# Even-layer attention heads: key low parts computed once, joined diagonals, a split pool of output-weight slabs and an earlier-issued gated product

## The chip, the cores and the metric

The kernel runs on one core of a Trainium2 chip. A core has a matrix engine (TensorE, PE in the profile), a vector engine (VectorE, DVE), a scalar engine (ScalarE, ACT), GpSimd (POOL) and a sync engine (SP) from which nearly all DMAs here are issued. Each engine works through its own instructions in a fixed order and waits on semaphores for the others. The metric is the device time of one launch in microseconds, taken as the median of the runs; lower is better. A profile of one execution stands beside it.

## The reference

Two layers over 512 tokens of width 1024 and 256 context tokens. Layer 0 is the "even" mixer with a feed-forward block, layer 1 the "odd" one with another. The change lies in the even mixer:

```python
def diff_attn(q, k, v, lam):                 # 4 heads, each with two score maps c = 0, 1
    s = jnp.einsum('bqhd,bkhd->bhqk', q, k).astype(jnp.float32) * ATTN_SCALE
    p = jax.nn.softmax(s, axis=-1).reshape(b, B_HEADS, 2, tq, tk)
    a = p[:, :, 0] - lam * p[:, :, 1]
    return jnp.einsum('bhqk,bkhe->bqhe', a.astype(v.dtype), v)

def diff_out(o, g, lam_init):
    return (rmsnorm(o, g) * (1.0 - lam_init)).reshape(b, t, B_V_WIDTH)

y = jnp.concatenate([chunk_mlp(u, v, w_s, b_s), diff_out(o, subln_g, lam_init)], axis=-1) @ w_out
```

The 512 tokens see 512 + 256 keys, the 256 context tokens see the 256 context keys only. `chunk_mlp` is a gated product: `u = gelu(h @ w)` times a mixed, normalized `gelu` of the other half. All is in float32.

## The kernel before

**Numbers in two parts.** Matrix products take operands rounded to a shorter float (F32R). So each operand is split into a rounded high part and a low part, the rest, and a product is three matmuls: high by high, high by low, low by high (`mm3`, lines 115 to 117). `split` and `unit` make the parts: ACT casts the high part, DVE or POOL subtracts it for the low part.

**The heads.** A score map has 64 channels, so high and low part of a query stand in the two halves of the 128 partitions of one tile (`stack_q`). The key tiles hold the same 64 channels in both halves: `stack_k` (line 281) makes a tile `kh` with the high part twice and a tile `kl` with the low part twice, and the score is query tile times `kh` plus query tile times `kl`. Each of the two maps of a head has its pair, so a head has four key tiles and four DVE subtractions (line 290) of 64 partitions by 768 columns. `softmax_diff` (line 537) does one block of 128 queries: two score maps into PSUM, a row maximum each (DVE, line 550), an exponential each (ACT, line 552, with the row sums), then on DVE the reciprocal, a factor (557), the difference of the two maps (558), and an epsilon term of the later norm, EPS times the squared sum (559). `attend` takes two such blocks, transposes them on PE (570), splits them into `ath` and `atl` (131, 132) and multiplies them with the values. A head has three `attend`, so six blocks. `norm` does the RMS norm of a head in steps: squares (ACT), sums by matmuls with ones and the reciprocal root on DVE with six small diagonal matrices (`rstd_diag`, lines 165 to 187), and a matmul that spreads the diagonals plus a scaling (615). The norm of head t-1 runs inside head t; that of head 3 stands at the end.

**What runs beside the heads.** The heads are traced with a high priority. PE's remaining time is filled with other products: `block` projects queries and keys of the later heads, with `rope` (line 260, DVE and POOL), and `gated` the four u products. Each `gated` is 24 matmuls over 512 columns and 24 over 256, into the one PSUM bank of `fill`. The framework orders each engine's instructions by priority along a timeline that it simulates; `issue_after(x)` forces an instruction behind `x` on its engine. For `gated(3, self.last_sum)` on line 704 all but the first two of the eight steps of the 512-column product (`dense`, `first = 2`) are put behind the last head's sums.

**What follows.** The weights `even_out` are loaded as eight slabs of 512 KB (`slab`, order 4, 5, 6, 0, 1, 2, 3, 7). Each takes a raw tile (three buffers), a cast on ACT (line 89) and a subtraction on POOL (line 92) into a slot of 8 KB per partition. All eight slots belong to one pool, opened after the ring of the earlier weights is closed; it reuses memory of the earlier ring, of the rope tables and of the attention tiles, and each tile waits until the tiles it lies on are released. The concatenated inputs `cat` are split in the same stretch into tiles that the inputs of `gated` held before. Then `xT` and `ctxT` are reloaded (line 43), the feed-forward weights begin to load (832), and `project(0, range(8), ...)` runs 24 matmuls for each slab in that order into eight accumulators.

Of the kernel before, what the change touches and what calls it, by code (L numbers as in the profile page):

```python
# [18 lines left out]
TC = 256  # L19
TA = TX + TC  # L20
HID = 2816
NF = HID // P
EPS = 1e-6
ROOT = 0.703952253
# [3 lines left out]
class Builder:  # L28
# [230 lines left out]

    def rope(self, ps, out, tabs):  # L260
        nc = self.nc
        sh = self.ropep.tile([P, 512], F32, name=self.uid("sh"), tag="sh", bufs=self.sh_bufs)
        nc.vector.stream_shuffle(sh, ps, ROT)
        nc.vector.tensor_tensor(out, ps, tabs[0], ALU.mult)  # L264
        nc.gpsimd.tensor_tensor(sh, sh, tabs[1], ALU.mult)
        nc.gpsimd.tensor_tensor(out, out, sh, ALU.add)
# [11 lines left out]
                nc.vector.scalar_tensor_tensor(lo[Y], q[X], s, hi[X].bitcast(F32), ALU.mult, ALU.subtract)  # L278
        return qa, qb

    def stack_k(self, k, pool, T, tag, bufs):
        nc = self.nc
        out = []
        for X, Y in ((slice(0, 64), slice(64, 128)), (slice(64, 128), slice(0, 64))):
            kh = pool.tile([P, T], F32R, name=self.uid("kh"), tag=tag, bufs=bufs)
            kl = pool.tile([P, T], F32R, name=self.uid("kl"), tag=tag, bufs=bufs)
            nc.scalar.copy(kh[X], k[X])
            nc.scalar.copy(kh[Y], k[X])
            for Z in (X, Y):
                nc.vector.tensor_tensor(kl[Z], k[X], kh[X].bitcast(F32), ALU.subtract)  # L290
            out.append((kh, kl))
        return out

# [39 lines left out]
    def even(self):  # L333
        tc, nc, a = self.tc, self.nc, self.a
        self.open_ring(512, 5, 6)
        self.ropep = tc.alloc_tile_pool(name="rope0", bufs=1, side="left", reuse_waits="tile")
        self.sh_bufs = 1
        self.ropep.tile([P, 512], F32, name=self.uid("sh"), tag="sh", bufs=1)
# [12 lines left out]
        for k in range(0, KT, 2):  # L351
            t = self.load(Rh, a["xT"][k * P:(k + 2) * P, :].rearrange("(k p) t -> p k t", p=P), [P, 2, TX], f"hx{k}")
# [47 lines left out]
        sq = self.squares(hx, TX)  # L400
        slabs = sum([ada_load(1, 1, k) for k in range(0, KT, 2)], [])
# [23 lines left out]
        qk = {}  # L425
# [37 lines left out]
        W = []  # L463
# [73 lines left out]
        def softmax_diff(Q, K, qb, eps):  # L537


            koff = 0 if qb < 4 else TX  # L540
            qs = slice(qb * P, (qb + 1) * P)
            nm, sums = self.small(2, "sa", 10), self.small(2, "sa", 10)
            es = []
            for c in range(2):
                ps = self.wide()
                for p in range(2):
                    if qb < 4:
                        nc.tensor.matmul(ps[:, :TX], Q[c][:, qs], K[c][p][:, :TX], start=p == 0, stop=p == 1)
                    nc.tensor.matmul(ps[:, TX:TA], Q[c][:, qs], K[c][p][:, TX:], start=p == 0, stop=p == 1)
                nc.vector.tensor_reduce(nm[:, c:c + 1], ps[:, koff:TA], axis=AX, op=ALU.max, negate=True)  # L550
                e = Ra.tile([P, TA], F32, name=self.uid("e"), tag="e", bufs=6)
                self.last_exp = nc.scalar.activation(e[:, koff:], ps[:, koff:TA], AF.Exp, bias=nm[:, c:c + 1],
                                                     accum_out=sums[:, c:c + 1])
                es.append(e[:, koff:])
            r = self.small(1, "sa", 10)
            nc.vector.reciprocal(r, sums[:, 1:2])
            nc.vector.scalar_tensor_tensor(r, r, self.nlam, sums[:, 0:1], ALU.mult, ALU.mult)
            nc.vector.scalar_tensor_tensor(es[0], es[1], r, es[0], ALU.mult, ALU.add)
            nc.vector.scalar_tensor_tensor(eps[:, qb:qb + 1], sums[:, 0:1], EPS, sums[:, 0:1], ALU.mult, ALU.mult)
            return es[0]  # L560

        def attend(t, Q, K, qp, o, eps):
# [21 lines left out]
        def gated(i, after=None):  # L584

            W = self.blocks(a["uv"][i])
            u = f3() if i < 4 else f3("rv")
            for off, T, A in ((0, TX, axx), (TX, TC, axc)):
                ps = (self.fill if off or i < 4 else self.bank)()[:, :T]
                self.dense(ps, W, A, after, 0 if off else 2)  # L590
                nc.scalar.copy(u[:, off:off + T], ps)
            raw[i] = u

        def stack(t):
            return (self.stack_q(qk[t], Ra, TA, "sq", 3, eng=nc.gpsimd if t == 3 else nc.vector),
                    self.stack_k(qk[4 + t], Ra, TA, "sk", 6))

        norms = {}

        def norm(t, step):  # L600

            if t not in norms:
                return
            o, eps = norms[t][:2]
            if step == 0:
                sq = self.sumsq()
                nc.scalar.activation(sq, o, AF.Square)
                norms[t] = o, eps, sq
            elif step == 1:
                sq = norms[t][2]  # L610
                norms[t] = o, eps, self.rstd_diag([(sq[:, :TX], TX), (sq[:, TX:], TC)], 1.0 / P, eps=eps)
            else:
                for off, T, dg in ((0, TX, norms[t][2][0]), (TX, TC, norms[t][2][1])):
                    c = o[:, off:off + T]
                    nc.vector.scalar_tensor_tensor(c, c, self.subg, self.spread(dg), ALU.mult, ALU.mult)

        def head(t):
            Q, K = QK.pop(t)
            o = f3("o", 4)
            eps = self.small(6, "sx", 2)  # L620
            for qp in range(3):
                attend(t, Q, K, qp, o, eps)
                if qp == 0:
                    norm(t - 1, 1)
                elif qp == 1:
                    if t < 3:
                        QK[t + 1] = stack(t + 1)
                    norm(t - 1, 2)
            norms[t] = o, eps
            norm(t, 0)  # L630
            if t == 3:
                norm(t, 1)
                norm(t, 2)
            oraw.append(o)
# [1198 lines left out]
```

## Time and profile before

| | us |
|---|---|
| median of three runs | 1580.58 |
| lowest, highest | 1578.69, 1582.02 |
| the profiled execution, whole | 1577.26 |
| its span in the profile | 1575.4 |

The profile names an instruction by line, engine, operation and tiles: `sa<-pw` reads a PSUM tile `pw` and writes a tile with the tag `sa`. In a table of windows each row gives a stretch of the span, the busy time of each engine in it, the clock granted to TensorE (1.00 is full speed) and the DMA share. In a table of groups, the two numbers behind the bar are the busy time of the group in all and the mean duration of one instruction in ns. In a timeline, the first number is the start, the second the duration, and the bracket gives the idle time before it and who ended it. The heads run from about 164 to 322 us, the last gated product and the first half of the output projection from there to about 373 us.

### The profile page before, as it was taken

How to read it: one execution, taken by the hardware profiler on the slowest of the kernel's cores; microseconds unless marked ns; L12 is line 12 of the kernel's file. 1: busy time of each engine (PE TensorE's matmuls, PEld its weight loads, DVE VectorE, ACT ScalarE, POOL GpSimd, SP SyncE). 2: the span in 40 equal slices, each digit the busy share in tenths (PEclk: the TensorE clock that was granted, in tenths of full speed). 3: DMA queues.
4: the chain of work that ended last, by engine and by line, in shares of the span. 5: the costliest groups of instructions: out<-in, count | busy, mean ns of one | idle time of the engine just before them, and what ended most of it. 6: DMA issues, size and time to landing. Idle time of an engine off the chain costs nothing.

```text
span 1575.4 us, 25009 instructions
## 1 busy us (share of the span) xinstructions
PE 1514.1 (96%) x9563; PEld 1354.2 (86%) x9563; DVE 1079.9 (69%) x1938; ACT 726.3 (46%) x1489; POOL 826.5 (52%) x558
## 2 busy tenths in 40 slices
PE   6999999889999999999999999999999999999998
PEld 4767888779999999999999988777879889999997
DVE  4613888853697787888886487665667966666665
ACT  2415566633653333333333354565655644444444
POOL 0452331041337767767776534541314399898982
PEclk9999999989999999999999999999999999999999
DMA  9772100042223333345442211210225133333201
GB/s 356 289 251 70 45 14 1 1 157 110 68 71 111 112 110 127 126 138 172 163 157 93 82 41 61 68 34 11 72 83 184 56 100 105 104 100 108 96 21 54
DMA packets 53415, 162.26 MB, mean 103 GB/s; under 512 B 6192, under 2 KB 8624, under 8 KB 45616
## 3 DMA queue, kind: packets, MB, share of 16 engines
q1 hardware_dynamic: 46240, 135.37, 25.3%
q10 hardware_dynamic: 7056, 25.30, 4.9%
q8 instruction: 75, 1.23, 0.3%
q14 instruction: 44, 0.36, 0.1%
HBM read 158.55 MB, written 2.10 MB: 102 GB/s over the span
## 4 chain that ended last, share of the span: by engine, by line
PE 79%; DVE 14%; ACT 2%; issue 2%; DMA 2%; POOL 0%; SPq 0%; DVEq 0%; ACTq 0%; POOLq 0%
PE pw L115 10%; PE pw L116 10%; PE pw L117 10%; PE pb L116 8%; PE pb L117 8%; PE pb L115 8%; PE pf L115 3%; PE pf L116 3%; PE pf L117 3%; PE pb L1643 2%; PE pb L1632 2%; PE pf L373 2%; PE pw L1594 1%; DMA raw<-even_out 1%; PE pw L1602 1%
## 5 line engine op out<-in xcount | busy, mean ns | idle before, releaser
L115 PE MATMUL pw<-ax,w 128*128 128x384 f32 (+2 forms) x716 | 227.4, 320 | 7.8 <-ACT w L89 4.2
L793 DVE SCALAR_TENSOR_TENSOR xT<-pb,mod,xT 128x512 f32<-128x512 f32 (+3 forms) x204 | 143.1, 709 | 129.2 <-PE pb L117 128.8
L116 PE MATMUL pw<-ax,w 128*128 128x384 f32 (+2 forms) x716 | 227.8, 318 | 3.5 <-DVE ax L49 2.2
L117 PE MATMUL pw<-ax,w 128*128 128x384 f32 (+2 forms) x716 | 227.4, 319 | 0.6 <-POOL w L92 0.3
L92 POOL TENSOR_TENSOR w<-raw,w 128x512 fp32r<-128x512 f32 (+1 forms) x78 | 116.2, 1496 | 196.7 <-ACT w L89 195.0
L49 POOL TENSOR_TENSOR w<-raw,w 128x512 fp32r<-128x512 f32 x122 | 185.4, 1535 | 48.9 <-ACT w L49 48.8
L49 POOL TENSOR_TENSOR w<-t,w 128x512 fp32r<-128x512 f32 x99 | 148.8, 1506 | 56.2 <-ACT w L49 56.2
L115 PE MATMUL pb<-hh,w 128*128 128x512 f32 x480 | 171.4, 357 | 1.2 <-DVE xT L793 1.2
L117 PE MATMUL pb<-hh,w 128*128 128x512 f32 x480 | 171.7, 358 | 0.0
L116 PE MATMUL pb<-hh,w 128*128 128x512 f32 x480 | 171.6, 357 | 0.0
L115 PE MATMUL pw<-T,w 128*128 128x384 f32 (+1 forms) x508 | 156.6, 310 | 2.5 <-DVE hs L999 1.2
L116 PE MATMUL pw<-T,w 128*128 128x384 f32 (+1 forms) x508 | 157.0, 310 | 1.2 <-DVE T L132 1.2
L117 PE MATMUL pw<-T,w 128*128 128x384 f32 (+1 forms) x508 | 157.0, 310 | 0.0
L115 PE MATMUL pf<-ax,w 128*128 128x256 f32 (+2 forms) x460 | 150.0, 326 | 1.1 <-DVE qf L264 1.1
L117 PE MATMUL pf<-ax,w 128*128 128x256 f32 (+2 forms) x460 | 148.5, 323 | 0.0
L116 PE MATMUL pf<-ax,w 128*128 128x256 f32 (+2 forms) x460 | 148.2, 322 | 0.0
L115 PEld LDWEIGHTS pw<-ax,w 128*128 128x128 f32 x716 | 136.0, 191 | 13.2 <-ACT w L89 5.0
L116 PEld LDWEIGHTS pw<-ax,w 128*128 128x128 f32 x716 | 136.7, 191 | 8.6 <-DVE ax L49 2.7
L117 PEld LDWEIGHTS pw<-ax,w 128*128 128x128 f32 x716 | 136.6, 191 | 3.7 <-POOL w L92 1.5
L49 POOL TENSOR_TENSOR hh<-hs,hh 128x768 fp32r<-128x768 f32 (+1 forms) x42 | 77.8, 1854 | 92.5 <-ACT hh L49 91.0
L49 POOL TENSOR_TENSOR w<-rawo,w 128x512 fp32r<-128x512 f32 x59 | 104.0, 1762 | 28.4 <-ACT w L49 28.4
L240 DVE SCALAR_TENSOR_TENSOR junk<-ar,cb 128x1024 bf16<-128x1024 f32 x64 | 106.8, 1668 | 0.0
(415 smaller groups left out, 3923.3 us busy)
## 6 DMA issues: line engine op xcount, KB each, us to landing
raw<-ffn_in SPq DMA_DIRECT2D x44, 1024.0 KB, 5.4
ar<-ada SPq DMA_DIRECT2D x24, 1024.0 KB, 6.7
ar<-ada ACTq DMA_DIRECT2D x48, 512.0 KB, 3.6
rawo<-ffn_out SPq DMA_DIRECT2D x88, 256.0 KB, 3.0
raw<-odd_out SPq DMA_DIRECT2D x28, 256.0 KB, 2.6
raw<-qk SPq DMA_DIRECT2D x16, 256.0 KB, 4.6
raw<-uv SPq DMA_DIRECT2D x16, 256.0 KB, 3.3
raw<-even_out SPq DMA_DIRECT2D x8, 512.0 KB, 4.9
```

Of the source, the lines that this page charges most:

```text
L49: self.tail[key] = fn(*args, **kw)
L92: eng.tensor_tensor(lo, raw, hi.bitcast(F32), ALU.subtract)
L115: mm(out, s[0], m[0], start=start, stop=False, **kw)
L116: mm(out, s[0], m[1], start=False, stop=False, **kw)
L117: return mm(out, s[1], m[0], start=False, stop=stop, **kw)
L240: return self.nc.vector.scalar_tensor_tensor(junk, t, 1.0, self.cb[who], ALU.mult, ALU.mult, accum_out=self.acc[who][:, col:col + 1])
L373: nc.tensor.matmul(ps[32 * q:32 * q + 32, :w], cst[:, k, :], t[:, w * q:w * q + w], start=k == 0, stop=k == KT - 1, skip_group_check=True)
L793: ins = self.nc.vector.scalar_tensor_tensor(h, ps[:, r], self.modcol(l, j, m, who), h, ALU.mult, ALU.add)
L1594: nc.tensor.matmul(ps[:, st:en], Q, K[g][p][:, b0 * P:b1 * P], start=p == 0, stop=p == 1, skip_group_check=True)
L1602: last = nc.tensor.matmul(ps[:, en:en + TC], Q, K[g][p][:, TX:], start=p == 0 and not edge, stop=p == 1, skip_group_check=True)
L1632: last = nc.tensor.transpose(pt[:, x * P:(x + 1) * P], es[2 * (x % 2) + x // 2][:, kb * P:(kb + 1) * P], self.ident)
L1643: nc.tensor.matmul(po[64 * h:64 * h + 64, :], V[vb][:, 64 * g:64 * g + 64], t[:, h * TC:h * TC + TC], start=kb == 0, stop=kb == nb - 1, sk ...
```

## The change

- `stack_k` computes each low part once, in the half of the partitions in which the query's high part stands; the other half, which met the query's low part, is zero, so the product of low by low is left out. The four `kl` tiles are allocated once for even and odd heads, their zero halves are written by four GpSimd memsets before the first head, and `kh` has three buffers of its own.
- The row sums of all six blocks of a head are kept in one tile of 12 columns. A new `head_diag` takes the place of `rstd_diag` in `norm`: one epsilon operation for all six blocks, a reciprocal root with two steps and tuned constants instead of three, and two diagonal operations with broadcast operands (four and two blocks) instead of six.
- In `gated(3, ...)` the first five of eight steps of the 512-column product are free of the order behind the last sums, instead of two.
- The eight slab slots are split: six in a pool `slabs`, two in the ring that also holds the raw tiles. The two are taken by the first two slabs. Both pools are released at the same place as before.
- `rope` uses a scratch tile of the shared tag "t" (two buffers) in the even layer instead of a tile of its own (one buffer), and `sgub` lies in a buffer of the tag "o".

```diff
-    def stack_k(self, k, pool, T, tag, bufs):
+    def stack_k(self, k, pool, T, tag, bufs, lows):
...
+        for X, Y, kl in zip((slice(0, 64), slice(64, 128)), (slice(64, 128), slice(0, 64)), lows):
             kh = pool.tile([P, T], F32R, name=self.uid("kh"), tag=tag, bufs=bufs)
-            kl = pool.tile([P, T], F32R, name=self.uid("kl"), tag=tag, bufs=bufs)
             nc.scalar.copy(kh[X], k[X])
             nc.scalar.copy(kh[Y], k[X])
-            for Z in (X, Y):
-                nc.vector.tensor_tensor(kl[Z], k[X], kh[X].bitcast(F32), ALU.subtract)
+            nc.vector.tensor_tensor(kl[X], k[X], kh[X].bitcast(F32), ALU.subtract)
...
-        sh = self.ropep.tile([P, 512], F32, name=self.uid("sh"), tag="sh", bufs=self.sh_bufs)
+        sh = self.ropep.tile([P, 512], F32, name=self.uid("sh"), tag="sh", bufs=2) if self.sh_bufs else self.tmp("t")
...
-            sgub = self.load(Rv, a["sgub"].partition_broadcast(P), [P, 512], "sgub")
+            sgub = f3("o", 4)[:, :512]
+            nc.sync.dma_start(sgub, a["sgub"].partition_broadcast(P))
...
-            nm, sums = self.small(2, "sa", 10), self.small(2, "sa", 10)
+            nm, sums = self.small(2, "sa", 10), sums[:, 2 * qb:2 * qb + 2]
...
-            nc.vector.scalar_tensor_tensor(eps[:, qb:qb + 1], sums[:, 0:1], EPS, sums[:, 0:1], ALU.mult, ALU.mult)
...
-                self.dense(ps, W, A, after, 0 if off else 2)
+                self.dense(ps, W, A, after, 0 if off else (2, 5)[i == 3])
...
+        lows = [[Ra.tile([P, TA], F32R, name=f"kl{i}{c}") for c in range(2)] for i in range(2)]
+        for i in range(2):
+            nc.gpsimd.memset(lows[i][0][64:128].bitcast(F32), 0.0)
+            nc.gpsimd.memset(lows[i][1][0:64].bitcast(F32), 0.0)
...
-                    self.stack_k(qk[4 + t], Ra, TA, "sk", 6))
+                    self.stack_k(qk[4 + t], Ra, TA, "kh", 3, lows[t % 2]))
...
+        def head_diag(sq, sums):
+
+            ve = nc.vector
+            v, y, u = self.small(6), self.small(6), self.small(6)
+            s0 = sums[:, :12].rearrange("p (n c) -> p n c", c=2)[:, :, 0]
+            ve.scalar_tensor_tensor(u, s0, EPS, s0, ALU.mult, ALU.mult)
+            for o, n in ((0, 4), (4, 2)):
+                ps = self.bank()
+                for j in range(n):
+                    c = slice(j * P, (j + 1) * P)
+                    self.last_sum = nc.tensor.matmul(ps[:, c], sq[:, (o + j) * P:(o + j + 1) * P], self.ones, start=j == 0,
+                                                     stop=True, skip_group_check=True)
+                col = ps[:, :n * P].rearrange("p (j f) -> p j f", f=P)[:, :, 0]
+                ve.scalar_tensor_tensor(v[:, o:o + n], col, 1.0 / P, u[:, o:o + n], ALU.mult, ALU.add)
+            ve.tensor_scalar(y.bitcast(I32), v.bitcast(I32), -0.5, float(0x5F1FFFF9), ALU.mult, ALU.add)
+            ve.tensor_tensor(u, y, y, ALU.mult)
+            ve.scalar_tensor_tensor(u, u, -1.0, v, ALU.mult, ALU.mult)
+            ve.scalar_tensor_tensor(y, u, 2.38924456, y, ALU.add, ALU.mult)
+            ve.tensor_tensor(u, y, y, ALU.mult)
+            ve.scalar_tensor_tensor(u, u, ROOT * ROOT, v, ALU.mult, ALU.mult)
+            ve.scalar_tensor_tensor(u, u, -10.0 / 3.0, u, ALU.add, ALU.mult)
+            ve.scalar_tensor_tensor(y, u, 5.0, y, ALU.add, ALU.mult)
+            dgs = []
+            for o, n in ((0, 4), (4, 2)):
+                dg = self.tmp()[:, :n * P]
+                self.last_diag = ve.scalar_tensor_tensor(
+                    dg.rearrange("p (j f) -> p j f", f=P), y[:, o:o + n].unsqueeze(2).to_broadcast([P, n, P]), 0.375 * ROOT,
+                    self.ident.unsqueeze(1).to_broadcast([P, n, P]), ALU.mult, ALU.mult)
+                dgs.append(dg)
+            return dgs
...
-        self.open_ring(1024, 3, 8)
-        slots = [self.slot() for _ in range(KT)]
+        self.slabs = tc.alloc_tile_pool(name="slabs", bufs=1, side="left", reuse_waits="tile")
+        slots = [self.slabs.tile([P, 2, 1024], F32R, name=self.uid("w"), tag="w", bufs=6) for _ in range(KT - 2)]
+        self.open_ring(1024, 3, 2)
+        slots += [self.slot() for _ in range(2)]
...
         self.close_ring()
+        if both:
+            self.slabs.release()
```

More of the change, by code (lines that the diff above doesn't have):

```diff
@@ L336, in even @@
         self.ropep = tc.alloc_tile_pool(name="rope0", bufs=1, side="left", reuse_waits="tile")
-        self.sh_bufs = 1
-        self.ropep.tile([P, 512], F32, name=self.uid("sh"), tag="sh", bufs=1)
+        self.sh_bufs = 0
         tabs = [self.ropep.tile([P, TX], F32, name=n, tag=n, bufs=1) for n in ("cos", "sin")]
@@ L535, in even, with softmax_diff @@
         oraw, raw = [], {}
-        def softmax_diff(Q, K, qb, eps):
+        def softmax_diff(Q, K, qb, sums):
             koff = 0 if qb < 4 else TX
             qs = slice(qb * P, (qb + 1) * P)
-            nm, sums = self.small(2, "sa", 10), self.small(2, "sa", 10)
+            nm, sums = self.small(2, "sa", 10), sums[:, 2 * qb:2 * qb + 2]
             es = []
@@ L610, in norm @@
                 sq = norms[t][2]
-                norms[t] = o, eps, self.rstd_diag([(sq[:, :TX], TX), (sq[:, TX:], TC)], 1.0 / P, eps=eps)
+                norms[t] = o, eps, head_diag(sq, eps)
             else:
@@ L619, in head @@
             o = f3("o", 4)
-            eps = self.small(6, "sx", 2)
+            eps = self.small(12, "sx", 2)
             for qp in range(3):
```

1 line of the change is left out of this document (removed).

## The prediction

> **What bounds the kernel now.** I read the page's head first, then the table of windows over the stretch that the change touches, then what TensorE waited for in it.
>
> ```profile
> span 1575.4 us, 25009 instructions
> PE 1514.1 (96%) x9563; PEld 1354.2 (86%) x9563; DVE 1079.9 (69%) x1938; ACT 726.3 (46%) x1489; POOL 826.5 (52%) x558
> ```
>
> TensorE is busy 96% of the span, and the change removes no matmul. So time can only come from TensorE's idle time and from stretches in which its clock is granted at half.
>
> ```profile
> 164.00:300.00 136.00, 127.59 (x816) 112.82 (x814) 121.69 (x280) 87.31 (x185) 32.14 (x22) 1.00 0.05 15
> 300.00:308.00 8.00, 6.52 (x49) 5.76 (x49) 6.71 (x27) 5.75 (x15) 0.00 (x0) 1.00 0.01 2
> 308.00:312.60 4.60, 0.78 (x4) 0.31 (x2) 3.92 (x8) 3.07 (x5) 0.00 (x0) 0.69 0.00 0
> 312.60:317.00 4.40, 4.40 (x15) 3.46 (x16) 2.15 (x10) 0.37 (x1) 0.00 (x0) 0.55 0.00 0
> 317.00:322.70 5.70, 3.35 (x25) 2.63 (x23) 1.88 (x4) 1.80 (x3) 0.00 (x0) 1.00 0.29 86
> ...
> 331.20:334.80 3.60, 0.03 (x1) 0.03 (x1) 2.45 (x2) 3.59 (x6) 2.68 (x3) 0.84 0.00 0
> 334.80:340.40 5.60, 5.60 (x18) 5.60 (x19) 5.60 (x3) 4.02 (x5) 5.60 (x2) 0.50 0.25 83
> 340.40:373.30 32.90, 31.80 (x176) 30.05 (x174) 8.64 (x6) 9.11 (x10) 16.88 (x7) 1.00 0.60 225
> 373.30:420.00 46.70, 46.70 (x277) 46.43 (x277) 29.91 (x76) 20.71 (x48) 14.56 (x12) 1.00 0.16 53
> ```
>
> Columns: stretch, length, busy time of TensorE, weight loads, VectorE, ScalarE, GpSimd, granted clock, DMA. Idle TensorE: 136.00 - 127.59 = 8.4 us up to 300, then 1.5, 3.8 and (317 to 322.7) 2.35, together 16.1 us in the heads; 3.6 us before the projection and 1.1 us in it. Clock: at 0.55 for 4.4 us about 2.0 us are lost, at 0.50 for 5.6 us 2.8 us. VectorE is busy 89% of the first stretch. From 373.3 TensorE has no idle time for 47 us, so what is won before then is not given back there.
>
> ```profile
> PE pb L116 <- DVE atl L132: 5.4, 7, 2.0
> PE pw L115 <- ACT w L89: 3.6, 1, 3.6
> PE pb L115 <- ACT ath L131: 3.5, 3, 2.5
> ...
> PE pb L668 <- DVE rv L669: 1.7, 1, 1.7
> ```
>
> These are TensorE's waits from 164 to 335 us (total, count, longest). The largest is for a VectorE operation, the low part of the transposed softmax; the second is a single wait, for the cast of the first output slab.
>
> **Part 1, VectorE's work in the heads.** Its groups from 164 to 322 us, and the two joined diagonals that already exist at the seam of the layers:
>
> ```profile
> L290 DVE TENSOR_TENSOR kl<-f,kh 64x768 fp32r<-64x768 f32 x12 | 12.4, 1031 | 0.5 <-ACT kh L287 0.3
> L559 DVE SCALAR_TENSOR_TENSOR sx<-sa 128x1 f32<-128x1 f32 x24 | 6.8, 285 | 0.8 <-ACT e L552 0.8
> ...
> L185 DVE TENSOR_SCALAR q<-ident,sm 128x128 f32<-128x128 f32 x18 | 3.8, 283 | 0.1
> ...
> L146 DVE TENSOR_TENSOR sm<-sm 128x6 f32<-128x6 f32 x9 | 2.5, 276 | 0.1
> ...
> L148 DVE SCALAR_TENSOR_TENSOR sm<-sm,sm 128x6 f32<-128x6 f32 x9 | 1.5, 162 | 0.1
> ...
> L147 DVE SCALAR_TENSOR_TENSOR sm<-sm,sm 128x6 f32<-128x6 f32 x9 | 1.4, 155 | 0.0
> ```
> ```profile
> L49 DVE SCALAR_TENSOR_TENSOR q<-sm,ident 128x512 f32<-128x512 f32 x1 | 0.7, 694 | 0.0
> ...
> L49 DVE SCALAR_TENSOR_TENSOR q<-sm,ident 128x256 f32<-128x256 f32 x1 | 0.4, 425 | 0.0
> ```
>
> Low parts: 6 of the 12 go, 6 x 1.03 = 6.2 us. Epsilon: 24 x 0.285 = 6.8 us become 4 operations of the six-column kind, 4 x 0.16 = 0.65 us; 6.2 us less. Root: ten small operations a head become eight; at the mean of their rows, (276 + 162 + 155) / 3 = 198 ns, that is 0.4 us, three norms in the stretch, 1.2 us. Diagonals: 3.8 us (18 that overlap one another) become 3 x (0.69 + 0.43) = 3.4; 0.4 us. Together 14 us of VectorE.
>
> [...]
>
> How much of 14 us reaches the end? At most TensorE's 8.4 us of gaps up to 300, at least nothing, because ScalarE's exponentials and casts stand in the same chain. The waits on `atl` and `rv` (7.1 us) are VectorE's, and removed operations stand in its queue ahead of them. I take 5 us, nearer the upper end. Bounds 0 and 8.4.
>
> **Part 2, the freed matmuls.** The gated product of index 3 after the last sums, first and last of 18:
>
> ```profile
> 322.68 0.48 PE L115 MATMUL pf<-ax,w 128*128 128x512 f32 x1
> ...
> 326.63 0.40 PE L117 MATMUL pf<-ax,w 128*128 128x512 f32 x1
> ```
>
> 18 matmuls in (326.63 - 322.68) x 18 / 17 = 4.2 us, so 0.232 us each. Nine of them may now run earlier: 2.1 us. The idle time from 300 to 322.7 is 7.65 us, so there is room. After the last sums only nine remain, and the second half of the product follows 2.1 us sooner. The diagonals must then be ready sooner too: two small operations fewer (0.4 us) and a first diagonal that no longer waits for four single ones cover about half of this, and the copy of the first half out of its bank covers the rest. I take 2.1 us. Below: if the nine stand in TensorE's queue ahead of scores that are ready, they delay the chain by 2.1 us, so -2.1. Above: if they break up the gaps after 308, the 2.0 us at half clock come on top, 4.1.
>
> [...] The trace has the clock at half after gaps of 2.46 and 1.36 us in a row (308 to 312.6), so here the measurement decides. [...]
>
> **Part 3, the slabs.**
>
> ```profile
> 319.89 1.28 SPq L86 DMA_DIRECT2D raw<-even_out  x3
> ```
> ```profile
> DMA to landing us min/median/max: 3.5/4.9/11.9
> ```
> ```profile
> 327.12 0.59 ACT L591 COPY f<-pf 128x512 f32<-128x512 f32 x1 [5.85 <-PE pf L117]
> ...
> 333.68 1.04 ACT L89 CAST w<-raw 128x1024 fp32r<-128x1024 f32 x1
> ```
>
> Three raw slabs are asked for at 319.89 and land within about 5 us (landing times of the `even_out` loads). ScalarE is idle for 5.85 us until 327.1 and yet casts the first slab at 333.68, after the gated product has ended. I read this as the slot: the eight slots reuse, among others, the memory of the ring whose weights the gated product still reads, and the first slab is given one of these. In the split pool the first two slabs have slots of their own above, on attention tiles, which are free about when the raw slabs come. Then both casts fit into ScalarE's gap and both subtractions on GpSimd begin some 9 us sooner, and the 3.6 us wait and the 2.8 us of half clock behind it go.
>
> But the end of this stage hangs on the last slab:
>
> ```profile
> 349.38 0.41 SPq L86 DMA_DIRECT2D raw<-even_out  x1
> ...
> 355.57 0.33 SPq L86 DMA_DIRECT2D raw<-even_out  x1
> ```
> ```profile
> 367.51 1.05 ACT L89 CAST w<-raw 128x1024 fp32r<-128x1024 f32 x1 [4.20 <-DMA raw<-even_out]
> ```
> ```profile
> SPq L43 <- DVE ax L132: 6.2, 1, 6.2
> ```
> ```profile
> L132 DVE TENSOR_TENSOR ax<-f,ax 128x768 fp32r<-128x768 f32 x4 | 11.6, 2945 | 1.9 <-ACT ax L131 1.9
> ...
> L725 DVE TENSOR_TENSOR f<-f,rv 128x768 f32<-128x768 f32 x1 | 0.9, 946 | 0.0
> ```
> ```profile
> L92 POOL TENSOR_TENSOR w<-raw,w 128x1024 fp32r<-128x1024 f32 x8 | 22.5, 2827 | 14.7 <-ACT w L89 14.7
> ```
>
> The sixth and eighth slab are issued at 349.38 and 355.57, behind the reloads of `xT`, whose memory SP gets only when VectorE has split the last inputs. Those subtractions take 2945 ns while GpSimd subtracts slabs at the same time; one of the same size, in the same stretch, takes 946. If two of GpSimd's (2 x 2.8 us) are done before, one or two of VectorE's run at the short price, 2 to 4 us. So the whole train of loads moves by about 3 us beyond parts 1 and 2, and with it the last cast. Upper bound: with no slab late, 192 matmuls at 32.9 / 190 = 0.173 us take 33.2 us from 331.2, ending at 364.4 in place of 373.3, 8.9 us. Lower bound 0, as TensorE just waits longer for the sixth to eighth slab. I take 3.
>
> **Edits at nothing.** Four memsets on GpSimd of 64 by 768:
>
> ```profile
> L357 POOL MEMSET cst<- 128x256 f32 x1 | 0.3, 317 | 0.0
> ...
> L265 POOL TENSOR_TENSOR sh<-sh,sin 128x512 f32<-128x512 f32 x18 | 25.2, 1403 | 59.9 <-DVE sh L263 38.7 <-DVE sa L556 9.6 <-DVE mv L655 8.0
> ```
>
> At 0.3 us (three times as many columns would be 1.0) to 1.4 us each they are 1.3 to 5.6 us, before the first scores at 164 and beside a GpSimd that is busy 32 of 136 us after that. Without this cover the first head would start by that much later. The rope's two shared buffers remove a wait of VectorE on GpSimd and add none that I find, since no other user of the tag runs in the heads. The move of `sgub` leaves its DMA in the same place of SP's queue; head 3's output takes that buffer over when the mixing has long read it.
>
> **The sum.** 5 + 2.1 + 3 = 10.1 us. The profiled execution took 1577.26, its span 1575.4, and the median of the runs is 1580.58, 3.3 us above it. The forecast is 1577.26 - 10.1 = 1567.2 on the profile's own scale and 1570.5 on that of the median. A difference under 0.2% (3.2 us) can't be told from no change.
>
> **The rivals.** (Times on the median's scale.)
>
> *The slabs gain nothing.* The slot was not what held the cast, or the last slab comes as late as before, and half of part 1 is hidden: 3 + 2 = 5 us, 1575.5. For it: the DMA stretch before the last slab is already full, and ScalarE's queue may place the casts where they are. Against: ScalarE's 5.85 us of idleness with the data landed.
>
> *All gaps close.* 8.4 + 4.1 + 6 = 18.5 us, 1562. For it: VectorE's removed 14 us exceed TensorE's gaps. Against: 3.5 us of waits are for ScalarE's `ath`, behind three GELUs that stay.
>
> *TensorE is not freed.* The chain runs through ScalarE as soon as VectorE is quicker, the freed matmuls only change places, and the slabs wait for DMA: about 2 us, 1578.6, no change.
>
> *The shared tile of sums makes it slower.* The exponential of a block writes its row sums into the tile that VectorE reads for the block before. If waits are placed by tile and not by column, 20 exponentials a run (five a head) queue behind VectorE's reciprocal and factor and one row maximum:
>
> ```profile
> L557 DVE SCALAR_TENSOR_TENSOR sa<-sa,nlam,sa 128x1 f32<-128x1 f32 x24 | 6.6, 276 | 0.3
> ...
> L550 DVE TENSOR_REDUCE sa<-pw 128x1 f32<-128x768 f32 x32 | 29.8, 947 | 6.6 <-PE pw L549 6.5
> ```
>
> At 0.16 (the reciprocal, priced like the small operations above) + 0.28 + 0.95 = 1.4 us that is 28 us on ScalarE; if half is behind other work, 14 us reach the end and eat the 10: 1584.5. It decides from 0.7 us a wait. Against: the old tiles with two columns already had this form, and no such wait shows.
>
> **How the numbers follow.** Forecast 45%, with a range of its own from 1566 to 1574; slabs gain nothing 25%; all gaps close 15%; not freed 10%; slower 5%. Faster by over 0.2% means below 1577.4: 45 + 15 + most of 25, 83%. Same: 10 + 2, 12%. Slower 5%. The range of 1562 to 1578 leaves out the slower case and parts of the two outer ones.
>
> **What would show it.** Part 1: 8 low-part operations instead of 16, four epsilon operations, and less than 5 us of idle TensorE between the start of the heads and the run of the last attention blocks. Part 2: nine 512-column matmuls after the last sums. Part 3: the first two slab casts ahead of the first copy of the gated product, no wait of the projection on the cast, clock 1.00 at its start, and the last slab cast earlier relative to the gated product's end. It is wrong if ScalarE's exponentials wait on reciprocals, if the projection's first matmul still waits over 2 us, or if the last slab's cast keeps its distance from the gated product's end.

## The result, and the profile after

The changed kernel takes 1576.61 us (median of 22 runs, 1574.61 to 1584.57), the kernel before, in the same series, 1580.16 (22 runs, 1577.03 to 1587.84). The ratio is 0.9977 with a 95% interval from 0.9966 to 0.9988: 0.0023 x 1580 = 3.6 us faster, between 1.9 and 5.4. The prediction had the sign right, and the time lies in its whole range of 1562 to 1578, but not in the forecast's own of 1566 to 1574: 10 us were forecast.

The two profiled executions don't lie at the same place of their series: 1582.97 for the changed kernel, 6.4 us above its median, and 1577.26 for the one before. So stages are compared below, not ends. Part of the 6.4 us is TensorE's granted clock: its mean over the whole of this execution is 0.990, that of the middle run of the series 0.993, and 0.003 x 1580 is 4.7 us. The mean clocks of the 22 executions lie between 0.987 and 0.994, so a clock below 1.00 in a row of this profile need not be there in every execution of the kernel. The page of the changed kernel begins:

```profile
span 1581.2 us, 24961 instructions
...
PE 1516.2 (96%) x9563; PEld 1357.0 (86%) x9563; DVE 1072.9 (68%) x1886; ACT 726.4 (46%) x1489; POOL 828.9 (52%) x562
```

The same number of matmuls, 52 VectorE instructions fewer. The table of windows of the changed kernel, columns as in the prediction:

```profile
164.00:300.00 136.00, 127.58 (x805) 113.77 (x804) 109.38 (x237) 84.80 (x177) 33.71 (x22) 0.97 0.05 15
...
334.80:340.40 5.60, 1.95 (x4) 0.92 (x5) 4.75 (x7) 1.20 (x2) 2.66 (x2) 0.85 0.69 272
340.40:373.30 32.90, 32.90 (x188) 32.72 (x188) 13.64 (x10) 12.75 (x15) 16.77 (x6) 0.97 0.58 208
```

Up to 300 us VectorE has lost 121.69 - 109.38 = 12.3 us of work and TensorE has not gained a hundredth: 127.59 before, 127.58 after. From 340 on TensorE is now busy without a gap, as hoped of the slabs. Just ahead of that, 334.8 to 340.4, it is busy 1.95 of 5.6 us, where the kernel before was busy all the time, at half clock (0.50). That hole is new. What VectorE (the last norm's root and diagonals), GpSimd and TensorE do there, from the timelines of the changed kernel (start, duration, instruction, idle time before it with its cause):

```profile
329.13 1.84 DVE L616 TENSOR_SCALAR sm<-sm 128x6 int32<-128x6 int32 x1
331.00 2.29 DVE L617 TENSOR_TENSOR sm<-sm 128x6 f32<-128x6 f32 x1
333.33 0.17 DVE L618 SCALAR_TENSOR_TENSOR sm<-sm,sm 128x6 f32<-128x6 f32 x1
333.53 0.17 DVE L619 SCALAR_TENSOR_TENSOR sm<-sm,sm 128x6 f32<-128x6 f32 x1
333.73 0.17 DVE L620 TENSOR_TENSOR sm<-sm 128x6 f32<-128x6 f32 x1
333.93 1.78 DVE L621 SCALAR_TENSOR_TENSOR sm<-sm,sm 128x6 f32<-128x6 f32 x1
335.75 1.73 DVE L622 SCALAR_TENSOR_TENSOR sm<-sm 128x6 f32<-128x6 f32 x1
...
337.71 1.03 DVE L627 SCALAR_TENSOR_TENSOR q<-sm,ident 128x512 f32<-128x512 f32 x2
```
```profile
328.54 4.74 POOL L92 TENSOR_TENSOR w<-raw,w 128x1024 fp32r<-128x1024 f32 x2 [42.92 <-PE pb L612]
333.88 3.58 POOL L132 TENSOR_TENSOR ax<-o,ax 128x768 fp32r<-128x768 f32 x2 [0.61 <-ACT ax L131]
```
```profile
338.45 1.86 PE L195 MATMUL pb<-q,ones 128*128 128x512 f32 x2 [4.23 <-DVE q L627]
```

Four of the eight root steps, each on six numbers a partition, take 1.7 to 2.3 us in place of 0.17. GpSimd's two pairs of subtractions run from 328.54 to 333.28 and from 333.88 to 337.46; the slow steps lie inside these two stretches, about as long as one of GpSimd's instructions each (4.74 / 2 = 2.37, 3.58 / 2 = 1.79), and the quick ones L618 to L620 begin in the break between them. The four take 7.64 us in place of 0.68, so the diagonals come 7 us late, and TensorE, in whose order the spread of the diagonal (L195) stands inside the second half of the gated product, stops for 4.23 us.

The slab casts themselves moved as predicted; ScalarE's timeline of the changed kernel, the first two ahead of the gated copy (333.68 and behind it before), and the last at 357.36 (367.51 before):

```profile
327.36 1.04 ACT L89 CAST w<-raw 128x1024 fp32r<-128x1024 f32 x1
328.62 1.05 ACT L89 CAST w<-raw 128x1024 fp32r<-128x1024 f32 x1 [0.22 <-DMA raw<-even_out]
331.06 0.59 ACT L588 COPY f<-pf 128x512 f32<-128x512 f32 x1 [1.39 <-PE pf L117]
...
357.36 1.05 ACT L89 CAST w<-raw 128x1024 fp32r<-128x1024 f32 x1 [3.50 <-DMA raw<-even_out]
```

And what TensorE waited for from 164 to 330 us, first in the changed kernel, then two rows of the kernel before that the prediction left out:

```profile
PE pw L546 <- ACT e L550: 5.7, 4, 2.6
PE pb L115 <- ACT ath L131: 4.7, 3, 3.8
...
PE pb L116 <- DVE atl L132: 1.6, 3, 0.7
...
PE pw L547 <- ACT e L550: 0.5, 1, 0.5
```
```profile
PE pw L549 <- ACT e L552: 1.9, 3, 0.9
...
PE pw L548 <- ACT e L552: 1.7, 2, 1.5
```

The waits for VectorE's low parts fell from 5.4 to 1.6 us. Those for the exponentials rose from 1.9 + 1.7 to 5.7 + 0.5, and those for ScalarE's casts from 3.5 to 4.7. The sum of these rows is 12.5 before and 12.5 after: in this execution TensorE waits as long as it did, for ScalarE instead of VectorE. Which part of the change moved them, the runs below tell.

### The profile page after: what moved, and what is told of

It is laid out like the page before. It is cut to its first block, busy times and chain, and to the rows that moved or that the text cites. A ratio compares the mean times of both kernels' runs of the same rounds, so it can differ in the third digit from the quotient of the medians.

```text
span 1581.2 us, 24961 instructions
## 1 busy us (share of the span) xinstructions
PE 1516.2 (96%) x9563; PEld 1357.0 (86%) x9563; DVE 1072.9 (68%) x1886; ACT 726.4 (46%) x1489; POOL 828.9 (52%) x562
## 4 chain that ended last, share of the span: by engine, by line
PE 84%; DVE 10%; ACT 3%; issue 2%; DMA 0%; POOL 0%; DVEq 0%; SPq 0%; ACTq 0%; POOLq 0%
PE pw L115 11%; PE pw L116 11%; PE pw L117 11%; PE pb L115 9%; PE pb L116 9%; PE pb L117 9%; PE pf L115 4%; PE pf L116 4%; PE pf L117 4%; PE pb L1680 2%; PE pb L1669 2%; PE pf L370 2%; PE pw L1631 1%; PE pw L1639 1%; DVE t L49 1%
```

## The experiments

Two theories, each with a rival. **T**: the slabs that come early harm the last norm, because GpSimd's subtractions run beside VectorE's root. **S**: in the heads the saving on VectorE is stopped by ScalarE's queue. All results, as ratio to the kernel before in the same series, and in us as (ratio - 1) x 1580; the last three columns are from one profiled execution each (start of the last sums, first output matmul, first residual operation):

| run | ratio, 95% interval | us | sums | output | residual |
|---|---|---|---|---|---|
| before | 1 | | 321.3 | 334.8 | 372.1 |
| changed | 0.9977 (0.9966 to 0.9988) | -3.6 | 327.3 | 342.0 | 372.5 |
| changed, again | 0.9978 (0.9963 to 0.9994) | -3.5 | 327.1 | 341.8 | 372.4 |
| casts held | 0.9943 (0.9926 to 0.9961) | -9.0 | 325.2 | 335.4 | 365.9 |
| first slabs on VectorE | 0.9948 (0.9929 to 0.9967) | -8.2 | 325.2 | 333.9 | 364.3 |
| split alone | 0.9964 (0.9948 to 0.9979) | -5.7 | 322.2 | 337.1 | 367.5 |
| no split | 0.9978 (0.9960 to 0.9996) | -3.5 | 327.1 | 338.8 | 373.8 |
| heads alone | 1.0005 (0.9990 to 1.0019) | +0.8 | 327.4 | 342.4 | 377.0 |
| freed matmuls alone | 0.9998 (0.9983 to 1.0013) | -0.3 | 324.4 | 337.2 | 374.1 |
| first slabs and key copies on VectorE | 0.9936 (0.9912 to 0.9959) | -10.1 | 324.3 | 332.9 | 363.3 |
| heads alone, key copies on VectorE | 0.9987 (0.9973 to 1.0002) | -2.1 | 323.0 | 336.5 | 371.5 |
| before, key copies on VectorE | 1.0033 (1.0020 to 1.0046) | +5.2 | 331.0 | 344.4 | 381.7 |
| split alone, first slabs on VectorE | 0.9949 (0.9930 to 0.9968) | -8.1 | 324.0 | 333.7 | 365.1 |
| fastest, matmuls not freed | 0.9953 (0.9936 to 0.9969) | -7.4 | 324.1 | 333.8 | 364.2 |

The columns of single executions scatter by some us; the verdicts rest on the ratios. An interval reaches 2 to 4 us to each side.

### The changed kernel again

No edit.

> The changed kernel once more, for a second profile of it. Theory T (the early slabs harm the last norm): in this profile too, the two-input steps of the last norm's root (multiply, multiply-add on six columns) take 1.7 to 2.3 us each instead of 0.16 to 0.17, because the two GpSimd subtractions of the first slabs run beside them, and TensorE waits about 4 us for the last diagonal in the middle of the gated product. Rival R (an accident of one execution): the steps take 0.2 us here and the wait is gone. Time by both: 1575 to 1578.

The first two root steps of the second execution, VectorE's timeline:

```profile
328.94 1.91 DVE L616 TENSOR_SCALAR sm<-sm 128x6 int32<-128x6 int32 x1
330.88 2.30 DVE L617 TENSOR_TENSOR sm<-sm 128x6 f32<-128x6 f32 x1
```

L621 and L622 follow with 1.74 and 1.73 us: the same four steps, and the same wait of TensorE (4.24 us). It is no accident of one execution. The ratio is that of the first series; its absolute median, 1580.71, stands beside 1583.46 for the kernel before, so medians of different series are not compared.

### The casts of the first slabs held

```diff
-                nc.scalar.copy(u[:, off:off + T], ps)
+                self.last_u = nc.scalar.copy(u[:, off:off + T], ps)
+                if not off:
+                    self.first_u = self.last_u
...
-        slab(0)
-        slab(1)
+        with tc.issue_after(self.first_u.ins):
+            slab(0)
+            slab(1)
```

> The changed kernel with one thing held: ScalarE's casts of slabs 0 and 1 (and with them GpSimd's two subtractions) come behind its copy of the first half of the gated product, as in the kernel before. Theory T: the root steps fall from about 2 us to 0.17 us, the diagonals are ready about 6 us sooner, and the wait of the gated product's second half for them goes; the head start of the two casts is given up in exchange, so the projection waits for its first slab again by 2 to 4 us. Sum: 0 to -3 us against the changed kernel, 1574 to 1577. Rival (the early casts are worth their 3 us and the slow steps have another cause): steps still about 2 us, time 2 to 4 us above the changed kernel.

VectorE's timeline of this run from the first root step to the diagonals, and ScalarE's around the copy:

```profile
328.35 0.17 DVE L618 TENSOR_SCALAR sm<-sm 128x6 int32<-128x6 int32 x1
...
329.76 0.17 DVE L625 SCALAR_TENSOR_TENSOR sm<-sm,sm 128x6 f32<-128x6 f32 x1
329.96 1.03 DVE L629 SCALAR_TENSOR_TENSOR q<-sm,ident 128x512 f32<-128x512 f32 x2
```
```profile
330.55 0.58 ACT L588 COPY f<-pf 128x512 f32<-128x512 f32 x1 [5.41 <-PE pf L117]
331.03 2.00 ACT L89 CAST w<-raw 128x1024 fp32r<-128x1024 f32 x2
```

All eight root steps take 0.17 us, and the diagonals begin 1.6 us after the first of them, not 8.6. GpSimd begins at 332.2, when the root is done. The ratio is 0.0035 below that of the changed kernel in the same series, 5.5 us. T gave 0 to 3 for it, with the projection waiting again for its first slab. It doesn't: the casts come 3.7 us later than in the changed kernel and still 4.4 us ahead of the first output matmul. The early start was worth nothing that shows here, and cost 5.5 us; the intervals of the two runs do not overlap.

### The first two slabs' low parts on VectorE

```diff
-        slab(0)
-        slab(1)
+        self.dve_lo = 1
+        with tc.issue_after(self.last_diag.ins):
+            slab(0)
+            slab(1)
+        self.dve_lo = 0
```

> The changed kernel with the low parts of slabs 0 and 1 subtracted by VectorE, behind the last diagonal, instead of by GpSimd beside the root. Theory T: root steps 0.17 us, diagonals some 6 us sooner, no wait of the gated product on them, and the first two slabs are still ready when the projection begins, since their casts are early and VectorE needs about 1.2 us for each: 3 to 5 us below the changed kernel, 1572 to 1574. Rival: the root is slow for another reason, or the projection just waits for its first slab instead: within 1 us of the changed kernel.

Its VectorE timeline; the casts stay early (325.18), and no GpSimd instruction runs beside the root:

```profile
327.03 0.17 DVE L616 TENSOR_SCALAR sm<-sm 128x6 int32<-128x6 int32 x1
...
328.64 1.03 DVE L627 SCALAR_TENSOR_TENSOR q<-sm,ident 128x512 f32<-128x512 f32 x2
329.58 2.35 DVE L92 TENSOR_TENSOR w<-raw,w 128x1024 fp32r<-128x1024 f32 x2
```

0.0030 below the changed kernel, 4.7 us, inside T's 3 to 5; all six runs (1574.17 to 1576.62) are below the changed kernel's median in this series, 1580.71. In the run with the casts held the timing of the casts moved with the subtractions; here only the engine of the subtractions (and the place behind the root) did, and the root is quick again, 0.17 us a step. It is GpSimd's subtractions that held it.

### The split alone, and with the first slabs on VectorE

The kernel before with the diff's pool `slabs` and nothing else of it; then with the edit of the run above as well.

```diff
-        self.open_ring(1024, 3, 8)
-        slots = [self.slot() for _ in range(KT)]
+        self.slabs = tc.alloc_tile_pool(name="slabs", bufs=1, side="left", reuse_waits="tile")
+        slots = [self.slabs.tile([P, 2, 1024], F32R, name=self.uid("w"), tag="w", bufs=6) for _ in range(KT - 2)]
+        self.open_ring(1024, 3, 2)
+        slots += [self.slot() for _ in range(2)]
...
         self.close_ring()
+        if both:
+            self.slabs.release()
```

> The kernel before with the split pool of slabs alone. Theory T: its casts of slabs 0 and 1 also go ahead of the gated product's copy, GpSimd's two subtractions then fall on the root of the last norm (here three steps of iteration on the same six columns), and what the early slabs win is lost there: 0 to -2 us against the kernel before. The prediction's part 3 as it stood: -3 us (-8.9 at most).

> The kernel before with the split pool and the low parts of slabs 0 and 1 on VectorE behind the last diagonal. Theory T: the two root steps that took 2.3 us in the run with the split alone take 0.17 us, the wait of 3.3 us for the diagonals goes, 2 to 4 us below that run, that is 7 to 9 us below the kernel before. Rival (the wait was covered by what follows): within 1 us of the split alone, 5 to 6 us below the kernel before.

Timelines of the run with the split alone, VectorE and TensorE:

```profile
325.63 2.33 DVE L147 SCALAR_TENSOR_TENSOR sm<-sm,sm 128x6 f32<-128x6 f32 x1
327.99 2.27 DVE L148 SCALAR_TENSOR_TENSOR sm<-sm,sm 128x6 f32<-128x6 f32 x1
```
```profile
331.22 2.88 PE L195 MATMUL pb<-q,ones 128*128 128x512 f32 x4 [3.33 <-DVE q L185]
```

Only the last two steps are caught, since GpSimd starts at 325.53, when the root is nearly done. So T erred in the sum: the split alone gains 5.7 us (3.3 to 8.2), more than T's 0 to 2 and more than the prediction's 3. Without the two slow steps it gains 8.1, as T expected; between the two runs, which are of different series, the intervals overlap. With the first slabs on VectorE the split by itself, without the other two parts, is as fast as the whole change with that edit (-8.1 and -8.2).

### The split undone

The lines of the diff just shown, reversed in the changed kernel.

> The changed kernel with the one ring of eight slots of the kernel before: the split alone undone. Its instructions stand in the same order on every engine as with the casts held, only the slots differ. Theory T (what the split brings is the early start, and that is what harms the root): steps at 0.17 us, no wait for the diagonal, first projection matmul at most 2 us later than with the casts held, 0 to 2 us above it: 1575 to 1577. Rival (the slot itself held the cast in the kernel before): casts again some 2.5 us behind the end of the gated product, projection waits 3.6 us, 3 to 5 us above the run with the casts held.

One thing in this expectation was wrong: the order is not that of the run with the casts held. ScalarE's timeline and TensorE's:

```profile
336.00 0.37 ACT L588 COPY f<-pf 128x256 f32<-128x256 f32 x1
336.27 0.83 ACT L131 CAST ax<-f 128x768 fp32r<-128x768 f32 x1
337.00 0.84 ACT L671 ACTIVATE f<-f 128x768 f32<-128x768 f32 x1
337.75 1.03 ACT L89 CAST w<-raw 128x1024 fp32r<-128x1024 f32 x1
```
```profile
338.83 0.69 PE L115 MATMUL pw<-ax,w 128*128 128x384 f32 x1 [2.87 <-ACT w L89]
```

With one ring the first cast stands behind the second copy, an input's cast and a GELU, one after the other: ScalarE works there and doesn't wait for a slot. The slot acts through the order that the framework writes from it. The projection waits 2.87 us again, and the ratio is 0.0035 above that of the run with the casts held (another series), 5.5 us, as the rival said, and a little more than its 3 to 5. So within the changed kernel the split is worth about 5.5 us, and its early subtractions take about as much away: with and without it the ratio is 0.998. That difference goes across two series, with intervals of 2 to 3 us to each side.

### The heads alone, and their key copies

The head part of the diff with one ring and without the freed matmuls. Then the same, and the kernel before, with one of two copies of each key tile on VectorE; and the run with the first slabs on VectorE with this edit too.

```diff
             nc.scalar.copy(kh[X], k[X])
-            nc.scalar.copy(kh[Y], k[X])
+            nc.vector.tensor_copy(kh[Y], k[X])
```

> The part of the change in the heads alone: low parts once, joined sums, eight-step root and two diagonals, with the one ring of slabs and without the freed matmuls. Theory S (TensorE's waits pass from VectorE to ScalarE, whose queue has the copies for the next head ahead of the exponentials): VectorE's busy time from 164 to 300 us falls by about 12 us, TensorE's by nothing, the waits of TensorE for VectorE's low parts fall by 4 us and those for exponentials rise by as much; 0 to -2 us against the kernel before. The prediction's part 1: -5 us.

> The part of the change in the heads alone, as in the run before it that gave no gain, with one of the two copies of each key tile's high part on VectorE instead of ScalarE. Theory S (VectorE's saving was stopped by ScalarE's queue at the change of heads): no wait for exponentials over 1.5 us there, clock 1.00 from 206 to 260 us, last sums 2 to 4 us sooner than without this edit; 2 to 4 us below the kernel before. Rival (the 12 us saved on VectorE were never on the path): within 1 us of the kernel before.

> The kernel before with only those copies moved from ScalarE to VectorE (16 copies of 64 by 768). Theory S (in the kernel before VectorE is the one that TensorE waits for): VectorE's busy time from 164 to 300 us rises by 3 to 6 us, TensorE's waits for its low parts rise, no gain: 0 to +3 us. Rival (moving the copies is a gain by itself, whatever VectorE does): -2 to -4 us.

> As the run with the first two slabs' low parts on VectorE, and in the heads one of the two copies of each key tile's high part goes from ScalarE (0.83 us) to VectorE, two a head. Theory S (ScalarE's queue holds the exponentials now): ScalarE's copies ahead of the exponentials fall by 1.7 us a head, TensorE's waits for exponentials by 2 to 4 us, time 1 to 3 us below the run with the slabs on VectorE alone, 1571.5 to 1573.5. Rival (the heads are held by something else, and VectorE's time is worth as much as ScalarE's): within 0.5 us of that run, or above it.

The heads alone: +0.8 us (-1.6 to +3.0). That is S's time, but only some of its signs came. Up to 300 us VectorE's busy time falls by 12.1 us (121.69 to 109.62) and TensorE's does not rise (127.59 to 127.24). TensorE's waits from 164 to 330 us:

```profile
PE pw L546 <- ACT e L550: 5.4, 3, 2.6
PE pb L116 <- DVE atl L132: 4.7, 7, 2.2
...
PE pw L547 <- ACT e L550: 0.4, 1, 0.4
```

The waits for the exponentials rise from 3.6 to 5.8 us, while those for VectorE's low parts fall by 0.7, not by the 4 that S had. ScalarE's queue where the second head begins, and TensorE's wait, in that run:

```profile
209.03 0.83 ACT L286 CAST kh<-f 64x768 fp32r<-64x768 f32 x1
209.89 0.83 ACT L287 CAST kh<-f 64x768 fp32r<-64x768 f32 x1
210.74 0.84 ACT L272 ACTIVATE qa<-f 64x768 fp32r<-64x768 f32 x1
211.49 0.45 ACT L550 ACTIVATE e<-pw,sa 128x256 f32<-128x256 f32 x1
```
```profile
212.09 0.80 PE L546 MATMUL pw<-kh,qa 128*128 128x512 f32 x1 [1.94 <-ACT e L550]
```

The exponential, which has to empty the bank for the next scores, stands behind copies of 0.83 us each for the following head. With the copy moved the two rows for the exponentials are 3.0 and 2.1 us: the longest wait falls from 2.6 to 1.4, the sum only from 5.8 to 5.1, and the row of the low parts stays (4.8). The clock is 1.00 up to 300 us (0.97 without), and the ratio is 0.9987: 2.1 us below the kernel before, inside S's 2 to 4, but the interval (-4.3 to +0.3) holds part of the rival's too.

The clearer answer is the same edit in the kernel before: 5.2 us slower (3.2 to 7.3), more than S's 0 to 3. It moves eight copies there (VectorE goes from 1938 instructions to 1946), not the sixteen of the expectation. One edit loses 5 us in the kernel before and nothing, or wins 3, after the change: VectorE's time is worth less in the heads than it was. How the 5 us are lost is open, since S's signs did not come: the waits for low parts are 5.2 us beside 5.4, and VectorE's busy time up to 300 us is 116.69 beside 121.69. TensorE does 4.9 us less in that stretch (122.71), and has new waits of 3.3 and 1.3 us for ScalarE to empty the bank `pf` of the other products.

In the run with both edits it goes 1.9 us on by the ratio (S: 1 to 3); the intervals of that and of its partner overlap. The waits for exponentials fall there from 6.2 to 5.6 us, where the expectation had 2 to 4 less, and those for low parts rise from 1.6 to 4.4. So that ScalarE's queue now holds the heads fits the times and the longest waits, but it is argued and not shown.

### The freed matmuls alone, and missing

```diff
-                self.dense(ps, W, A, after, 0 if off else 2)
+                self.dense(ps, W, A, after, 0 if off else (2, 5)[i == 3])
```

> The kernel before with nine more matmuls of the gated product freed, nothing else. The prediction's part 2: nine matmuls fewer behind the last sums, 2.1 us, all of it gained: -2 us. Theory S: the matmuls fall into TensorE's waits in the last head, so the last sums come no later than before and the gain is the whole 2 us, unless the first diagonal, which then has only 2.1 us of other work ahead of it, is late: then 0 to -1 us, with a wait of TensorE on the diagonals of 1 to 2 us.

> The fastest version so far (changed kernel, first slabs' low parts on VectorE, one copy per key tile on VectorE) with the nine matmuls of the gated product not freed. If the freed matmuls are worth their 2.1 us once nothing waits behind them: 2 us above that version, 1572 to 1573. If they only stand ahead of the last head's own matmuls: within 0.7 us of it.

Alone they give -0.3 us (-2.7 to +2.1). TensorE's timeline at the spread:

```profile
329.16 1.12 PE L195 MATMUL pb<-q,ones 128*128 128x512 f32 x2 [1.10 <-DVE q L185]
```

With nine matmuls less behind the sums the six single diagonals are 1.1 us late, the smaller case that the expectation named. In the profiled execution the last sums come at 324.4, 3.1 us later than in that of the kernel before, which is more than the 2.1 us that went ahead of them. In the fastest version, leaving them out costs 2.7 us by the ratios (0.9953 against 0.9936), of different series, with intervals of 3 us and more: not told apart.

One pair of runs of the same series does tell them apart. The run with the split undone is the heads with the freed matmuls, the heads alone are the same without them: the medians are 1578.93 and 1582.52, 3.6 us, and ten of the twelve runs with them are below the fastest one without (1580.1). TensorE's waits for low parts are 1.6 us in the one and 4.7 in the other, and from 300 us on, in the last head, 0.3 and 3.3. There the matmuls do fill waits, as part 2 of the prediction had it, and with the shorter root TensorE has no wait of 1.1 us for the diagonals.

## Why the prediction was wrong

**Part 3, forecast 3 us.** The reading was right in what it saw: ScalarE's idle time, the casts that move ahead of the gated copy, the last slab's cast 10 us sooner, the wait of 3.6 us gone. Alone it measures 5.7, without GpSimd's disturbance 8.1, near the upper bound of 8.9. The step that failed is the sentence that "both subtractions on GpSimd begin some 9 us sooner", put down as pure gain. The prediction had the price in its own fence: VectorE's subtractions at 2945 ns beside GpSimd's, and one operation of the same size at 946, begun 0.18 us ahead of GpSimd's (334.62 and 334.80 us; with GpSimd idle, at 308.68 us in the kernel before, another takes 0.96 us). It used that pair for the inputs that would get cheaper and didn't ask what stands on VectorE at the place to which GpSimd's work was moving. It was the last norm's root, the one chain that TensorE waits for. In the changed kernel four steps were caught, and 5 us lost.

The traces show how long the steps are held: a step on six numbers takes 2.29 us beside a GpSimd instruction of 2.37 in the changed kernel and 2.33 beside one of 2.35 with the split alone, and 0.17 where GpSimd is idle beside the root (casts held, first slabs on VectorE). By what mechanism GpSimd holds them is not shown by any run.

**Part 1, forecast 5 of 8.4 us.** The work removed was counted nearly right (14 forecast, 12.3 measured up to 300 us). The joined diagonals won 0.24 us a norm, more than the 0.1 that the prediction's 0.4 for three norms comes to: the two take 1.03 us, the six single ones of the kernel before 1.27. What failed is the share that reaches the end: alone it measures nothing. The working gave the reason itself, that "ScalarE's exponentials and casts stand in the same chain", and then chose the upper half since the waits on `atl` and `rv` are VectorE's. That reading failed: with the heads changed alone, these 7.1 us fell by 0.7. The wait on `rv` is 1.7 us as before, and that on `atl` 4.7 in place of 5.4, while the waits for exponentials rose by 2.2. The prediction's own sign, less than 5 us of idle TensorE, was missed: 8.4 us up to 300 as before. In the whole change the waits for `atl` fell by 3.8 us, but 2.5 of that lie behind 300 us (2.8 to 0.3), where the freed matmuls fill in; 3.8 us came back as waits for ScalarE, in fewer and longer pieces.

The clock may add to it. Up to 300 us it is 0.97 in six of the nine profiles with the new heads, 0.99 in one, and 1.00 in two, both with the key copies on VectorE; but the last run of the table has these copies too and 0.97. In the five with the old heads it is 0.99 or 1.00. One execution each doesn't settle whether the change brings that loss.

**Part 2, forecast 2.1 us.** Alone nothing. In that run the diagonals are 1.1 us late, which the prediction had covered by two steps fewer and a joined diagonal; those belong to part 1. With them the freed matmuls are worth 3.6 us in one series, inside the prediction's bound of 4.1. So the step that failed here is the adding up: part 2 was forecast as a gain of its own, and it needs part 1. Parts 1 and 2 together, without the split, measure -3.5 (-6.3 to -0.6). With the split and without the disturbance they add nothing to it (-8.2 against -8.1, of two series). What the two are worth in that company is not settled.

**The rivals.** The one named "TensorE is not freed" said what happened in the heads and in the last product, at 10%; its third clause, on the slabs, was wrong. "The slabs gain nothing" came nearest in time, 5 us, by causes that the runs refute. The slower one didn't come: ScalarE's waits for VectorE are still those for the row maximum (24.7 us after, 27.9 before), and none for reciprocal or factor is listed. The row of the changed kernel:

```profile
ACT e L550 <- DVE sa L548: 24.7, 21, 2.7
```

**The memsets**, at nothing, took 4 x 0.74 us on GpSimd; no wait for them is among TensorE's or ScalarE's in the heads.

So the sum of the change is: a split that is worth 5.5 us in its company, early subtractions that take 5.5 back, and 3.5 us of the other two parts together, 2.1 + 5 in the forecast. The run with the first slabs' low parts and the key copies on VectorE reaches 0.9936 of the kernel before, 10 us. That is the number that was forecast, but by another road, and so no support for the forecast.

## What to carry to other kernels

When a change starts work on GpSimd earlier, look up what VectorE runs in that new place, at its own instruction lengths: in a chain of tiny operations there a step can cost a whole GpSimd instruction (here up to 2.33 us in place of 0.17), and if TensorE waits for that chain, the early start is a loss. Time saved on an engine counts only up to the point where the next wait ends: change each part alone and read the same rows of waits again, since a row that fell in the whole change may have fallen for another part of it. To see whether an engine's time still counts, put the same work on it before and after the change. A transfer or cast needs to be early enough, not as early as it can be: begun 4.4 us before its use, the first slab's cast kept nothing waiting here.

## What the runs showed of the hardware

A VectorE operation of one input, the integer step L616, was held too, not only those with two: it took 1.84 and 1.91 us beside GpSimd in the two profiles of the changed kernel, and 0.17 with the first slabs on VectorE.

After the same idle time TensorE's clock was halved in one execution (0.51) and not in another (1.00). The windows around a wait of 1.94 us that ends at 212 us, with 3.1 of the 6 us before it idle, first the run of the heads alone, then the run with the first slabs on VectorE, whose heads are the same there:

```profile
206.00:212.00 6.00, 2.90 (x19) 2.10 (x17) 5.46 (x9) 5.88 (x10) 0.00 (x0) 0.92 0.00 0
212.00:218.00 6.00, 5.91 (x24) 5.53 (x25) 5.25 (x11) 2.87 (x9) 1.28 (x1) 0.51 0.00 0
```
```profile
206.00:212.00 6.00, 2.87 (x18) 2.04 (x16) 5.46 (x9) 5.88 (x10) 0.00 (x0) 1.00 0.00 0
212.00:218.00 6.00, 5.96 (x44) 5.68 (x45) 5.93 (x12) 4.57 (x11) 2.26 (x2) 1.00 0.00 0
```

The clock is 0.51 in one for six microseconds, some 3 us of work, and 1.00 in the other. That may be a part of why single executions of one kernel lie 5 to 10 us apart; no run here was made to show it.
